# All of w_down in groups 0 to 5 by seven products, with the rows' scale put on at the residual

## The chip, the cores and the metric

The kernel runs on one core of a Trainium2 chip. The core has a TensorE (PE) for matmuls, a VectorE (DVE), a ScalarE (ACT), a GpSimd (POOL), a SyncE (SP) that issues transfers, and 16 DMA engines. The metric is the device time of one execution in microseconds (us). Three timed runs of the kernel before took 1994.78 to 1995.85 us, with a median of 1994.91.

## The reference

Two layers of a transformer-like trunk over 256 tokens (rows) of 2048 features. Each layer has an attention part and then the MLP that this change is about:

```
def rmsnorm(x, g):
    return x * lax.rsqrt(jnp.mean(x * x, axis=-1, keepdims=True) + EPS) * g

h = rmsnorm(x, norm_mlp[l])
u = jax.nn.relu(jnp.einsum('bsd,df->bsf', h, w_up[l]))        # w_up: 2048 x 8192
x = x + jnp.einsum('bsf,fd->bsd', u * u, w_down[l])           # w_down: 8192 x 2048
```

The factor rsqrt(mean + EPS), called r here, is one number per token. Since it is positive, relu(r * a) squared is r * r * relu(a) squared, so r may be applied before the square or, as its square, to any sum over the 8192 units.

## The kernel before

**Precision.** All data are float32. A weight tile is split into hi + lo: ACT casts it to a rounded form (whi, L1036), DVE subtracts that from the weights (wlo, L1037), and PE multiplies with hi and with lo. Activations are split in the same way, so a plain product of a tile takes three parts: hi x hi, lo x hi and hi x lo. All of the text calls one weight tile of 128 x 1024 numbers (512 KB) with its transfer, its cast, its DVE split and its matmuls a *step*. Three whi and three wlo buffers go round, and five for raw weights (wraw). Weight transfers are issued on SP seven steps ahead (LOOK_LOAD), splits two steps ahead (LOOK_SPLIT).

**The MLP in groups.** The 8192 units are taken in eight groups of 1024. An *up step* holds a part of w_up: eight matmuls of 128x512 with whi (L675), eight of 128x256 with wlo (L680). Four up steps make one column of 256 units, and a group has four columns, so 16 up steps, U0 to U15 below. After a column's last step `evac` in `up_steps` brings it out: ACT copies half of each bank (L653), DVE adds the other half (L654), DVE takes relu and multiplies with a row of r's (L655), ACT squares (L658) and casts (L660), DVE forms the lo part (L661). The row of r's, `rrow`, is made once per layer by `rows` in `mlp_rs`: two DVE operations, matmuls with a matrix of ones (L505) and a copy (L506). Because it comes late, a step's `post` defers the first column's evac by a step. `sums_of` makes sums and differences of the units' parts for the products (L696 to L701).

**Seven products for eight.** `strassen_steps` multiplies a group's units with two 512-column halves of w_down in the way of Strassen-Winograd: seven products P1 to P7 (in the order P1, P2, P7, P6, P5, P3, P4) of sums of weight blocks with sums of unit blocks. Every product runs over two weight tiles, called its first and second tile below; such a *product step* is six matmuls of 128x512 (L806). The operands are made in place: `on_top` is a GpSimd transfer that adds a block of w_down onto a tile in SBUF (L792), `sum_of` is a DVE sum of two tiles (L788). The tiles are `side` (four buffers), `spare` (one each of two) and `big`. DVE adds each finished bank to the residual x (L777), or subtracts it. A bank is made ready by the evacuation before: a new product can't start in a bank that is not yet added.

**Groups 0 to 5.** Columns 0 to 1023 of w_down (pair 0) are done by fourteen product steps. Columns 1024 to 2047 (pair 1) are done by seven product steps on the first tiles, and the second tiles' part by four plain *down steps* (`down_steps`) of twelve matmuls each (L468), whose banks DVE adds at L728. All of it runs beside the 16 up steps of the next group. The list `order` sets how the two kinds (1 for w_down's products, 0 for the others) follow each other; in the group's second half the products and the others alternate, and the list ends with two of the others. Groups 6 and 7 are done otherwise and keep their form.

**What sets the order on an engine.** Each engine executes its instructions in a fixed order, made when the program is built from the order in which the code issues them and a scheduler's costs. Waits between engines are semaphores. POOL issues the accumulating transfers one after the other: a later one waits while an earlier one is waiting for its tile.

Of the kernel before, what the change touches and what calls it, by code (L numbers as in the profile page):

```python
# [25 lines left out]
L = 2  # L26
# [17 lines left out]
def tile_trunk(ctx: ExitStack, tc: tile.TileContext, x_in, xt_in, w_in, w_o, w_up, w_down,  # L44
# [4 lines left out]
    D_X, D_S, D_SS, D_T, D_PV, D_QK, D_RQ, D_RK, D_SQ, D_R = 6.0, 6.0, 7.0, 18.0, 6.0, 6.0, 24.0, 16.0, 6.0, 4.0  # L49
# [52 lines left out]
    rrow = cp.tile([P, 256], F32, name="rrow")  # L102
# [350 lines left out]
    class Step:  # L453


        def __init__(self, src, kk, n, pre, mm, fourth=True, loads=None, prep=None, raw=None, post=None,
                     look=LOOK_PREP):
            self.look = look
            self.src, self.kk, self.n, self.pre, self.mm, self.fourth = src, kk, n, pre, mm, fourth
            self.loads, self.prep, self.raw, self.post = loads or [], prep, raw, post  # L460
# [27 lines left out]
    def layer_steps(l):  # L488
# [6 lines left out]
        def mlp_rs():  # L495
            r = rsqrt(mean_eps(st["ss2"], 4, 1.0 / D), 2)

            def rows():

                dg = mid(F32, 2, P)  # L500
                for t in range(NT):
                    nc.vector.tensor_scalar(dg[:, t, :], ident, r[:, t:t + 1], None, op0=ALU.mult)
                ps = tr_bank()
                for t in range(NT):
                    nc.tensor.matmul(ps[:, t * P:(t + 1) * P], full, dg[:, t, :], start=True, stop=True)  # L505
                nc.vector.tensor_copy(rrow, ps[:, 0:256])  # L506
                flags.add(("rrow", l))
            add(rows, 0.45, delay=D_R, front=True)
# [133 lines left out]
        def up_steps(g):  # L642

            out_, evacs = [], []
            for q in range(4 * g, 4 * g + 4):
                box = {}

                def evac(q=q, box=box):
                    need(("rrow", l))
                    a = mid(F32, 2, 256)  # L650
                    for i in range(2):
# [3 lines left out]
                    nc.vector.scalar_tensor_tensor(  # L655
                        a, a, 0.0, rrow.rearrange("p (o c) -> p o c", o=1).to_broadcast([P, 2, 256]),
                        op0=ALU.max, op1=ALU.mult)
# [7 lines left out]
                for s in range(4):  # L665
# [3 lines left out]
                    def mm(wh, wl, s=s, q=q, box=box, evac=evac):  # L669
# [12 lines left out]
                        if s == 3 and q > 0:  # L682
                            evac()

                    out_.append(Step(w_up[l, q * 4 + s], 4, 256, pre, mm, fourth=False,
                                     post=evacs[0] if (q, s) == (1, 0) else None))
                    if s == 0:
                        evacs.append(evac)
# [15 lines left out]
        def down_steps(gs, j, ks=range(4), shared=None):  # L704

            out_, box = [], {}
            tiles = [(g, k) for g in gs for k in ks]  # L710
# [525 lines left out]
```

## Time and profile before

| | |
|---|---|
| median of three runs | 1994.91 us |
| the profiled execution | 1995.7 us |
| its span | 1993.9 us |
| one group of 0 to 5 in the trace | 84.57 to 84.69 us |
| up steps, product steps and plain down steps in it | 16, 21, 4 |

The page of the profile gives for each engine its busy time, the share of the span and the number of instructions; PEld is PE's loading of weights, which overlaps its matmuls. A row of a timeline gives the start in us from the span's start, the duration, the engine, line and operation, output<-input with the buffers' names, and in brackets the idle time before it and what ended that. A row of a group has its count after the x, and then the sum in us, the mean in ns of one, and the idle time before it. Instructions overlap their neighbours a little, so that what one costs on its engine is read from start to start.

### The profile page before, as it was taken

How to read it: one execution, taken by the hardware profiler on the slowest of the kernel's cores; microseconds unless marked ns; L12 is line 12 of the kernel's file. 1: busy time of each engine (PE TensorE's matmuls, PEld its weight loads, DVE VectorE, ACT ScalarE, POOL GpSimd, SP SyncE). 2: the span in 40 equal slices, each digit the busy share in tenths (PEclk: the TensorE clock that was granted, in tenths of full speed). 3: DMA queues.
4: the chain of work that ended last, by engine and by line, in shares of the span. 5: the costliest groups of instructions: out<-in, count | busy, mean ns of one | idle time of the engine just before them, and what ended most of it. 6: DMA issues, size and time to landing. Idle time of an engine off the chain costs nothing.

```text
span 1993.9 us, 28351 instructions
## 1 busy us (share of the span) xinstructions
PE 1980.3 (99%) x10134; PEld 1683.2 (84%) x10134; DVE 1647.0 (83%) x2197; ACT 1247.4 (63%) x1778; POOL 396.4 (20%) x462
## 2 busy tenths in 40 slices
PE   9999999999999999999999999999999999999998
PEld 7888888888888888888888888888888888888887
DVE  6777877888888888888857678778988988888887
ACT  7667756666565656566656677566666656656664
POOL 0674620001010010100008745201010001101000
PEclk9999999999999999999999999999999999999999
DMA  9755755888888888978666467568898988989884
GB/s 341 212 164 153 235 168 190 224 260 260 252 256 243 273 248 251 273 224 252 207 190 201 153 177 222 169 190 251 233 273 243 269 248 247 265 252 260 238 264 126
DMA packets 128635, 456.31 MB, mean 229 GB/s; under 512 B 14660, under 2 KB 16964, under 8 KB 128493
## 3 DMA queue, kind: packets, MB, share of 16 engines
q1 hardware_dynamic: 109052, 384.18, 56.4%
q0 software_dynamic: 19008, 69.21, 20.1%
q8 instruction: 80, 1.31, 0.3%
q10 hardware_dynamic: 432, 1.10, 0.1%
q14 instruction: 63, 0.51, 0.1%
HBM read 448.65 MB, written 2.11 MB: 226 GB/s over the span
## 4 chain that ended last, share of the span: by engine, by line
PE 96%; DVE 1%; DMA 1%; ACT 1%; issue 1%; SPq 0%; POOL 0%; POOLq 0%; DVEq 0%; ACTq 0%
PE mm L468 32%; PE mm L675 23%; PE S L806 18%; PE mm L680 12%; PE mm L806 3%; PE S L468 2%; PE tr L380 1%; PE tr L399 1%; DMA wraw<-in_w_in_dram 1%; PE S L343 1%; PE S L342 1%; PE tr L223 1%; DVE wlo L1037 0%; ACT big L360 0%; PE tr L392 0%
## 5 line engine op out<-in xcount | busy, mean ns | idle before, releaser
L1037 DVE TENSOR_TENSOR wlo<-wraw,whi 128x1024 fp32r<-128x1024 f32 (+1 forms) x517 | 634.3, 1233 | 200.9 <-ACT whi L1036 191.4
L1036 ACT CAST whi<-wraw 128x1024 fp32r<-128x1024 f32 (+1 forms) x517 | 541.2, 1051 | 360.2 <-PE mm L675 100.2
L675 PE MATMUL mm<-big,whi 128*128 128x512 f32 x2048 | 514.1, 390 | 0.0
L468 PE MATMUL mm<-whi,big 128*128 128x512 f32 (+1 forms) x1692 | 500.1, 384 | 0.8 <-ACT whi L1036 0.8
L675 PEld LDWEIGHTS mm<-big,whi 128*128 128x128 f32 x2048 | 380.5, 188 | 79.4 <-ACT whi L1036 2.2
L468 PEld LDWEIGHTS mm<-whi,big 128*128 128x128 f32 x1692 | 314.3, 188 | 61.8 <-ACT whi L1036 1.9
L680 PEld LDWEIGHTS mm<-big,wlo 128*128 128x128 f32 x2048 | 280.9, 190 | 21.2
L468 PE MATMUL mm<-wlo,big 128*128 128x512 f32 (+1 forms) x846 | 293.3, 382 | 0.0
L806 PE MATMUL S<-whi,big 128*128 128x512 f32 x1056 | 290.1, 396 | 0.0
L680 PE MATMUL mm<-big,wlo 128*128 128x256 f32 x2048 | 287.3, 282 | 0.0
L806 PEld LDWEIGHTS S<-whi,big 128*128 128x128 f32 x1056 | 184.3, 189 | 34.2 <-DVE x L777 2.8
L468 PEld LDWEIGHTS mm<-wlo,big 128*128 128x128 f32 x846 | 159.3, 188 | 28.7
L806 PE MATMUL S<-wlo,big 128*128 128x512 f32 x528 | 163.4, 391 | 0.0
L1036 ACT CAST whi<-side 128x1024 fp32r<-128x1024 f32 x88 | 92.5, 1051 | 85.3 <-PE mm L675 76.6
L1036 ACT CAST whi<-big 128x1024 fp32r<-128x1024 f32 x88 | 92.9, 1056 | 77.5 <-DVE big L788 27.7
L468 PE MATMUL mm<-spare,big 128*128 128x512 f32 (+1 forms) x606 | 140.2, 380 | 0.0
L1037 DVE TENSOR_TENSOR wlo<-side,whi 128x1024 fp32r<-128x1024 f32 x88 | 107.7, 1224 | 35.4 <-ACT whi L1036 34.6
L792 POOL DMA_DIRECT2D spare<-in_w_down_dram x44 | 38.1, 866 | 476.2 <-DVE wlo L1037 458.4
L468 PEld LDWEIGHTS mm<-spare,big 128*128 128x128 f32 x606 | 108.9, 188 | 20.4
L1037 DVE TENSOR_TENSOR wlo<-big,whi 128x1024 fp32r<-128x1024 f32 x88 | 107.7, 1224 | 21.5 <-ACT whi L1036 21.3
L792 POOL DMA_DIRECT2D side<-in_w_down_dram x44 | 38.3, 881 | 400.9 <-DVE mid L654 150.8
L806 PEld LDWEIGHTS S<-wlo,big 128*128 128x128 f32 x528 | 99.2, 188 | 22.2
(163 smaller groups left out, 2310.3 us busy)
## 6 DMA issues: line engine op xcount, KB each, us to landing
wraw<-in_w_up_dram SPq DMA_DIRECT2D x256, 512.0 KB, 4.8
wraw<-in_w_down_dram SPq DMA_DIRECT2D x124, 512.0 KB, 5.1
wraw<-in_w_in_dram SPq DMA_DIRECT2D x119, 512.0 KB, 3.7
side<-in_w_down_dram SPq DMA_DIRECT2D x88, 512.0 KB, 5.2
wraw<-in_w_o_dram SPq DMA_DIRECT2D x64, 512.0 KB, 3.7
side<-in_w_down_dram POOLq DMA_DIRECT2D x44, 512.0 KB, 7.5
spare<-in_w_down_dram SPq DMA_DIRECT2D x44, 512.0 KB, 5.9
spare<-in_w_down_dram POOLq DMA_DIRECT2D x44, 512.0 KB, 5.5
```

The costliest lines, as they stand in the source:

```text
L223: nc.tensor.transpose(psv[:, kk, t, :], x[:, t, c0:c0 + P], ident)
L342: nc.tensor.matmul(o, st, u.kh[:, kh, :], start=True, stop=False)
L343: nc.tensor.matmul(o, st, u.kl[:, kh, :], start=False, stop=True)
L380: nc.tensor.transpose(ps[:, c * P:(c + 1) * P], u.p[:, s, kb * P:(kb + 1) * P], ident)
L399: nc.tensor.matmul(ps, u.V[:, kb, u.kv, :, :], pt[:, kb, :], start=n == 0, stop=n == 3)
L468: nc.tensor.matmul(banks[t][:, 0:n], a, (wl if part == "hl" else wh)[:, i, :], start=first and i == 0 and part == "hh", stop=last and i == ...
L675: nc.tensor.matmul(box["b"][fs], wh[:, kk, fs * P:(fs + 1) * P], ht, start=s == 0 and kk == 0, stop=False, skip_group_check=True)
L680: nc.tensor.matmul(box["b"][fs][:, 0:256], wl[:, kk, fs * P:(fs + 1) * P], ht[:, 0:256], start=False, stop=s == 3 and kk == 3, skip_group_ ...
L792: nc.gpsimd.dma_start(tile, src(par, j, h).rearrange("p (k n) -> p k n", k=2), accum_op=ALU.add)
L806: nc.tensor.matmul(o, ops[i][a], w[:, i, :], skip_group_check=True, start=fresh and h == 0 and i == 0 and a == 0 and w is wh, stop=h == ti ...
L1036: last_act[0] = nc.scalar.copy(h[:, part], w[:, part]).ins
L1037: last_lo[0] = nc.vector.tensor_sub(lo[:, part], w[:, part], f(h[:, part])).ins
```

## The change

There are two parts.

First, in groups 0 to 5 columns 1024 to 2047 are done by fourteen product steps too, for the seven product steps and the four plain steps. `_pack_down` packs the weights for it, on the host, as the packing before did for pair 0. For this second pair `moved` is empty: P7's operand, B12 + B22, is a DVE sum of two loaded tiles instead of an accumulating transfer, on both tiles. The `order` list puts a step of the other kind between the two tiles of each product but the last, and three more of them after products 1, 5 and 9 of the group.

Second, the row of r's and its matmuls are gone. The units are squared without a scale: relu moves from DVE to ACT (`AF.Relu`), the `post` deferral is dropped, and r * r, one number per row, is made once per layer on GpSimd with its negative (`r2`). Every bank of w_down is brought into the residual by `scaled_add`, x = bank * r2 + x, one DVE operation for the add or subtraction before.

```diff
         def mlp_rs():
-            r = rsqrt(mean_eps(st["ss2"], 4, 1.0 / D), 2)
-            def rows():
-                dg = mid(F32, 2, P)
-                for t in range(NT):
-                    nc.vector.tensor_scalar(dg[:, t, :], ident, r[:, t:t + 1], None, op0=ALU.mult)
-                ps = tr_bank()
-                for t in range(NT):
-                    nc.tensor.matmul(ps[:, t * P:(t + 1) * P], full, dg[:, t, :], start=True, stop=True)
-                nc.vector.tensor_copy(rrow, ps[:, 0:256])
-                flags.add(("rrow", l))
-            add(rows, 0.45, delay=D_R, front=True)
+            nc.gpsimd.tensor_tensor(r2[:, l, 0], mean_eps(st["ss2"], 4, 1.0 / D), mone[:, 0:NT], op=ALU.pow)
+            nc.gpsimd.tensor_scalar(r2[:, l, 1], r2[:, l, 0], -1.0, None, op0=ALU.mult)
...
                 def evac(q=q, box=box):
-                    need(("rrow", l))
...
-                    nc.vector.scalar_tensor_tensor(
-                        a, a, 0.0, rrow.rearrange("p (o c) -> p o c", o=1).to_broadcast([P, 2, 256]),
-                        op0=ALU.max, op1=ALU.mult)
+                    nc.scalar.activation(a, a, AF.Relu, bias=zero1[:, 0:1])
                     nc.scalar.activation(a, a, AF.Square, bias=zero1[:, 0:1])
...
+        def scaled_add(xs, bank, t, sign=1):
+            col = r2[:, l, (1 - sign) // 2, t:t + 1]
+            nc.vector.scalar_tensor_tensor(xs, bank, col, xs, op0=ALU.mult, op1=ALU.add)
...
-                xs = x[:, t, 1024 * pair + j * 512:1024 * pair + (j + 1) * 512]
-                op = nc.vector.tensor_add if sign > 0 else nc.vector.tensor_sub
-                op(xs, xs, bank)
+                scaled_add(x[:, t, 1024 * pair + j * 512:1024 * pair + (j + 1) * 512], bank, t, sign)
...
                     elif name == "P7":
+                        if h not in moved:
+                            loads = [(("B12", h), src(0, 1, h), None), (("B22", h), src(1, 1, h), None)]
+
                         def prep(h=h):
-                            on_top(raw["B12", h], 1, 1, h)
+                            if h in moved:
+                                on_top(raw["B12", h], 1, 1, h)
+                            else:
+                                sum_of(raw["B12", h], raw["B12", h], raw["B22", h])
...
             if g < 6:
-                up = up_steps(g + 1)
-                ss = up[0:4] + down_steps((g,), 3, (2, 3)) + up[4:]
-            elif g == 6:
-                ss = up_steps(7)
-            else:
-                ss = down_steps((6, 7), 2) + down_steps((6,), 3) + down_steps((7,), 3)
-            hs, _ = strassen_steps(g)
-            if g < 6:
-                more, shared = strassen_steps(g, 1, (0,), 4)
-                hs += more
-
-            if g < 6:
+                hs += strassen_steps(g, 1, ())
                 order = []
-                for p_ in range(7):
-                    order += [1, 0, 1] + [0] * (p_ in (0, 1, 2, 4))
-                order += [0, 1] * 7 + [0, 0]
-                ss += down_steps((g,), 2, (2, 3), shared)
+                for p_ in range(14):
+                    order += [1, 0, 1] if p_ < 13 else [1, 1]
+                    order += [0] * (p_ in (0, 4, 8))
```

The lines of the changed kernel that answer to those above: casts L1015, splits L1016, sums L769, accumulating transfers L773, evacuations of products L689, copies L642, adds L643, Relu L644, Square L645, cast of units L647.

Over the whole program the order listings count 72 matmuls of 128x512 and four of 128x128 fewer, 36 more casts and 36 more splits of weights, 36 more DVE sums (80 for 44), 64 Relus on ACT for 64 relu-and-scale operations on DVE, 24 evacuations of banks fewer (207 for 231), and 144 accumulating transfers for 132. Transfers issued by SP are the same in number.

Three places of the engines' orders follow. The first is ACT at the end of a group. Before, the rows run from a plain down step's cast over the copies of the last up column; `whi_5297` belongs to U0 of the next group, `spare_5189` and `spare_5224` are the two tiles of its P1:

```order
L1036 CAST whi_5265<-wraw_5176 128x1024
L653 COPY mid_5246<-mm_5125 128x256
L653 COPY mid_5246<-mm_5126 128x256
L1036 CAST whi_5279<-spare_5189 128x1024
L1036 CAST whi_5297<-wraw_5211 128x1024
L658 ACTIVATE mid_5246<-mid_5246,zero_88 128x512
L660 CAST big_5253<-mid_5246 128x512
L1036 CAST whi_5319<-spare_5224 128x1024
```

Now `big_5027` and `big_5063` are the operands of P4's two tiles, `whi_5311` belongs to U0, `spare_5218` and `spare_5243` are P1's tiles:

```order
L1015 CAST whi_5245<-big_5027 128x1024
L1015 CAST whi_5284<-big_5063 128x1024
L642 COPY mid_5265<-mm_5114 128x256
L642 COPY mid_5265<-mm_5115 128x256
L1015 CAST whi_5299<-spare_5218 128x1024
L644 ACTIVATE mid_5265<-mid_5265,zero_88 128x512
L645 ACTIVATE mid_5265<-mid_5265,zero_88 128x512
L647 CAST big_5272<-mid_5265 128x512
L1015 CAST whi_5311<-wraw_5231 128x1024
L1015 CAST whi_5326<-spare_5243 128x1024
```

U0's cast stood ahead of the Square, and now stands behind Relu, Square and the cast of the units.

The second is DVE where the second pair's P7 and P6 are prepared. Before (`side_4946` is P7's operand, `big_5072` P6's):

```order
L1037 TENSOR_TENSOR wlo_5056<-side_4946,whi_5055 128x1024
L1037 TENSOR_TENSOR wlo_5069<-wraw_4997,whi_5068 128x1024
L788 TENSOR_TENSOR big_5072<-side_5019,spare_4894 128x1024
L654 TENSOR_TENSOR mid_5090<-mid_5090,mm_4967 128x256
L654 TENSOR_TENSOR mid_5090<-mid_5090,mm_4968 128x256
L655 SCALAR_TENSOR_TENSOR mid_5090<-mid_5090,rrow 128x512
L1037 TENSOR_TENSOR wlo_5108<-big_5072,whi_5107 128x1024
```

Now (`side_4969` and `side_5007` are P7's operands, `big_5027` and `big_5063` P6's, which P4 uses later):

```order
L1016 TENSOR_TENSOR wlo_5012<-wraw_4942,whi_5011 128x1024
L769 TENSOR_TENSOR side_4969<-side_4969,side_4971 128x1024
L1016 TENSOR_TENSOR wlo_5024<-wraw_4956,whi_5023 128x1024
L769 TENSOR_TENSOR big_5027<-side_4971,spare_4842 128x1024
L1016 TENSOR_TENSOR wlo_5048<-side_4969,whi_5047 128x1024
L769 TENSOR_TENSOR side_5007<-side_5007,side_5009 128x1024
L689 SCALAR_TENSOR_TENSOR x<-mm_5016,r_83,x 128x512
L1016 TENSOR_TENSOR wlo_5060<-wraw_4994,whi_5059 128x1024
L769 TENSOR_TENSOR big_5063<-side_5009,spare_4893 128x1024
```

One sum stood there; now four stand among the splits.

The third is POOL, whose rows here are accumulating transfers alone. Before, over the end of a group:

```order
L792 DMA spare_4894<-in_w_down_dram 128x1024
L792 DMA big_5072<-in_w_down_dram 128x1024
L792 DMA spare_5189<-in_w_down_dram 128x1024
L792 DMA spare_5224<-in_w_down_dram 128x1024
L792 DMA side_5717<-in_w_down_dram 128x1024
```

Now, where `big_5805` and `big_5841` are the operands of P4's two tiles and `side_6073` and `side_6100` belong to the next group's P7:

```order
L773 DMA spare_5620<-in_w_down_dram 128x1024
L773 DMA spare_5671<-in_w_down_dram 128x1024
L773 DMA side_6073<-in_w_down_dram 128x1024
L773 DMA big_5805<-in_w_down_dram 128x1024
L773 DMA side_6100<-in_w_down_dram 128x1024
L773 DMA big_5841<-in_w_down_dram 128x1024
L773 DMA spare_5996<-in_w_down_dram 128x1024
```

The second pair's accumulations onto `big` now stand behind those onto the next group's `side` tiles.

69 lines of the change are left out of this document (32 added, 37 removed).

## The prediction

> **What bounds the kernel now.** I read the page's busy times and its chain first, then the stretches by group, then the timelines of PE, ACT and DVE at the end of a group. The page:
>
> ```profile
> PE 1980.3 (99%) x10134; PEld 1683.2 (84%) x10134; DVE 1647.0 (83%) x2197; ACT 1247.4 (63%) x1778; POOL 396.4 (20%) x462
> PE 96%; DVE 1%; DMA 1%; ACT 1%; issue 1%; SPq 0%; POOL 0%; POOLq 0%; DVEq 0%; ACTq 0%
> ```
>
> The chain that ended last is 96% matmuls. The stretches table for two of the twelve groups that the change touches (columns: busy time and count on PE, weight loads, DVE, ACT, POOL, then clock, DMA share, GB/s):
>
> ```profile
> 380.10:464.72 84.62, 84.62 (x432) 71.84 (x431) 74.43 (x94) 51.73 (x62) 7.75 (x9) 1.00 0.87 255
> 464.72:549.41 84.69, 84.69 (x432) 71.87 (x431) 74.43 (x94) 51.72 (x62) 7.77 (x9) 1.00 0.87 254
> ```
>
> PE is busy for the whole of each group at the full granted clock. So a removed matmul is worth its own time for as long as the operands keep coming. DVE has 10.2 us to spare per group and is the next bound; ACT has 33. What steps cost on PE, from the chain and the timeline of PE:
>
> ```profile
> 464.72 2.72 PE mm L468 x12
> 397.87 1.98 PE L675 MATMUL mm<-big,whi 128*128 128x512 f32 x8
> 399.68 1.11 PE L680 MATMUL mm<-big,wlo 128*128 128x256 f32 x8
> 400.63 1.09 PE L806 MATMUL S<-whi,big 128*128 128x512 f32 x4
> 401.56 0.62 PE L806 MATMUL S<-wlo,big 128*128 128x512 f32 x2
> 402.02 1.29 PE L675 MATMUL mm<-big,whi 128*128 128x512 f32 x5
> ```
>
> A 128x512 matmul takes 2.72/12 = 0.227 us. From start to start, an up step is 1.81 (hi) + 0.95 (lo) = 2.76 us and a product step 402.02 - 400.63 = 1.39 us.
>
> **What the change removes on PE.** Per group of 0 to 5, seven product steps of six matmuls and four plain steps of twelve (90) become fourteen product steps (84): 6 x 0.227 = 1.36 us. Over 12 groups that is 16.3 us. The scale's row, once per layer, goes too:
>
> ```profile
> 325.00 0.60 PE L505 MATMUL tr<-mid,full 128*128 128x128 f32 x4
> 325.37 1.86 PE L675 MATMUL mm<-big,whi 128*128 128x512 f32 x7
> ```
>
> That is 325.37 - 325.00 = 0.37 us, twice 0.7. The group end before has a short wait, on DVE's evacuations of the plain steps' banks (PE rows, then DVE rows):
>
> ```profile
> 446.35 1.75 PE L675 MATMUL mm<-big,whi 128*128 128x512 f32 x7
> 448.05 1.20 PE L806 MATMUL S<-whi,big 128*128 128x512 f32 x4
> ...
> 449.77 1.10 PE L680 MATMUL mm<-big,wlo 128*128 128x256 f32 x8
> ...
> 447.31 0.68 DVE L728 TENSOR_TENSOR x<-x,S 128x512 f32<-128x512 f32 x1
> ```
>
> From the first to the last row of PE stand eight hi matmuls and one product step: 449.77 - 446.35 = 3.42 us, where 1.81 + 1.37 is 3.18. So 0.24 us is waiting; the product starts when the evacuation of its bank ends (447.31 + 0.68). With the plain steps gone this goes, at ten group ends (five per layer; groups 5 to 6 join differently): 2.4 us.
>
> **What it adds on DVE and ACT.** Durations, from DVE's timeline and the groups table:
>
> ```profile
> 392.54 1.22 DVE L1037 TENSOR_TENSOR wlo<-wraw,whi 128x1024 fp32r<-128x1024 f32 x1
> 393.67 0.68 DVE L777 TENSOR_TENSOR x<-x,S 128x512 f32<-128x512 f32 x1
> 394.27 1.22 DVE L1037 TENSOR_TENSOR wlo<-spare,whi 128x1024 fp32r<-128x1024 f32 x1
> ...
> 423.40 0.75 DVE L654 TENSOR_TENSOR mid<-mid,mm 128x256 f32<-128x256 f32 x2
> ...
> 310.18 1.40 DVE L633 SCALAR_TENSOR_TENSOR x<-mm,sm,x 128x512 f32<-128x512 f32 x2
> ```
> ```profile
> L788 DVE TENSOR_TENSOR big<-side,spare 128x1024 f32<-128x1024 f32 x44 | 53.6, 1219 | 0.0
> L655 DVE SCALAR_TENSOR_TENSOR mid<-mid,rrow 128x512 f32<-128x512 f32 x64 | 44.0, 687 | 0.7
> L658 ACT ACTIVATE mid<-mid,zero 128x512 f32<-128x512 f32 x64 | 46.2, 722 | 15.2 <-DVE mid L655 15.2
> ```
>
> A split occupies DVE for 393.67 - 392.54 = 1.13 us, an evacuation for 0.60; a sum has the duration of a split, so 1.13 too. The scaled evacuation is the form of L633, bank times a column plus x: it is not seen on a product's bank, but bounded by 0.60 (no dearer than the add) and by 0.70 (two in 1.40); I take 0.66. Per group: three more splits and three more sums, 6 x 1.13 = 6.8; evacuations from 16 x 0.60 to 14 x 0.66, -0.4; four Relu-and-scale operations leave, 4 x 0.60 = -2.4. Together +4.0: DVE goes from 74.4 to about 78.4 of a group of 83. On ACT three casts at 0.95 and four Relus at the Square's 0.722: +5.7, to 57 of 83. Neither bounds on average. The two GpSimd operations per layer and the removed deferral of the first evacuation are done while up steps with 2.76 us each of matmuls run; from nothing to twice 0.4 us, I take nothing.
>
> **Where a new wait comes: the end of a group.** The new order puts the last two products' steps together: P3's second tile, both tiles of P4, then the next group's first up step U0, with no up step between. On ACT, U0's cast now stands behind the Relu, the Square and the cast of the last up column; before, U0's cast stood ahead of the Square. Durations and hops, from PE's and ACT's timelines:
>
> ```profile
> 463.17 1.09 PE L806 MATMUL S<-whi,big 128*128 128x512 f32 x4
> ...
> 463.38 0.64 ACT L653 COPY mid<-mm 128x256 f32<-128x256 f32 x2
> ...
> 466.57 1.06 ACT L1036 CAST whi<-big 128x1024 fp32r<-128x1024 f32 x1 [1.22 <-PE mm L468]
> 467.52 0.72 ACT L658 ACTIVATE mid<-mid,zero 128x512 f32<-128x512 f32 x1
> 468.28 0.62 ACT L660 CAST big<-mid 128x512 fp32r<-128x512 f32 x1
> 468.81 1.05 ACT L1036 CAST whi<-wraw 128x1024 fp32r<-128x1024 f32 x1
> ```
>
> A copy starts 463.38 - 463.17 = 0.21 us after the matmuls it reads. On ACT a Square takes 0.76 to the next start, the cast of units 0.53, a cast of weights 0.95. Walk, with zero at the end of P3's first tile on PE. The last up step's lo matmuls end at 0.95; P3's second tile at 2.33, P4's two at 3.70 and 5.07 (1.37 to 1.39 each): there PE wants U0. DVE: the split for P4's first tile waits for the lo buffer that P3's first tile holds, so 0.2 to 1.34; the second tile's 1.34 to 2.47; only then the two adds of the up column, 0.75 for both, to 3.22. (The copies are done at 1.8; the adds are queued behind the splits.) ACT: Relu 3.25, Square 4.0, cast of units 4.76, U0's cast 5.29 to 6.34. PE waits 6.4 - 5.07 = 1.3 us. Behind U0's split DVE has P4's evacuation, and the next group's first product needs that bank: about 0.1 more. So 1.4 us at each of ten ends, 14 us. Bounds: nothing, if ACT gets to Relu before the splits; 1.9, if hops of 0.2 come in at three places of the chain. I take the walk, since every item of it has its row. Queued behind U0's cast on ACT is only P1's second cast, which PE wants 4.1 us later.
>
> At groups 5 to 6 the new order has two up steps in front and U0's cast ahead of the chain; I count no stall there.
>
> **The sum.** The profiled execution took 1995.7 us (span 1993.9), 0.8 over the median of 1994.91. 1995.7 - 16.3 - 0.7 - 2.4 + 14 = 1990.3; less 0.8 is 1989.5 us. Its own range, with stalls of 0.9 to 1.9 at an end: 1984.5 to 1994.5.
>
> **Rivals.**
> *Full gain.* If ACT takes U0's cast in time (the adds run ahead, or the lo buffer comes free sooner than walked), there is no stall: 1989.5 - 14 = 1975.5. For it: PE did not stall in 84.62 us of these groups but for the 0.24. Against: the order of ACT's queue, which is fixed.
>
> *A late accumulate (slower).* Each group gains one accumulating GpSimd DMA, ten for nine. The window's DMA queues and issues (median us from issue to landing at the end):
>
> ```profile
> q0 software_dynamic: 1296, 4.72, 32.4%
> side<-in_w_down_dram SPq DMA_DIRECT2D x6, 512.0 KB, 4.9
> side<-in_w_down_dram POOLq DMA_DIRECT2D x3, 512.0 KB, 8.3
> big<-in_w_down_dram POOLq DMA_DIRECT2D x3, 512.0 KB, 6.7
> ```
>
> The accumulate that makes the operand of P4's second tile is now queued on POOL behind one into the next group's side tile, whose load waits until P7's second tile is split. From there to the P4 cast PE does eight product and three up steps, 8 x 1.38 + 3 x 2.76 = 19.3 us; cast and split must lie 3.5 us ahead and P7's split lies about 1 ahead of its own, so 16.8 us. Needed: load 4.9, two issues of about 0.9, landing 6.7, three hops of 0.2 to 0.4: 14.3. The margin is 2.5 us: late from a landing of 9.2 us on, and each us beyond costs 1 us in 12 groups. One more accumulate at a ninth of 32.4% brings the DMA share from 0.87 to 0.91. A landing of 11.5 us would be 2.3 x 12 = 28 us over the forecast, less what overlaps with the stall at the end: about 2010. Against: the longest queue's median here is 8.3.
>
> *DVE's burst (slower).* The second pair's four sums (P7 and P6, both tiles) now stand within six splits. DVE there: (4 + 6) x 1.13 + 0.66 + 0.75 = 12.7 us; PE's steps for these six splits: 4 x 1.39 + 2 x 2.76 = 11.1. If DVE comes to the burst without a lead, 1.6 us per group is lost, 12 x 1.6 = 19: 2009; were all three added sums uncovered, 3 x 1.13 x 12 = 41: 2030. Against: splits run up to two steps ahead, and by my walk 0.9 us of the lead is left.
>
> *DVE as the bound throughout (slower).* If DVE's queue can't be filled beyond the share that it has now, 74.43/84.62 = 88%, then 78.4 us of work take 89.1 us per group, 4.5 more than before: 1994.9 + 12 x 4.5 = 2049. Against: PE is busy for 84.62 of 84.62, which a DVE bound would not leave. The Trainium skill, "Perfetto Trace Analysis", section "Identifying the Most-Contended Engine", states that matmul busy time is no measure of TensorE's headroom, that its weight-load share is, and that the engine with the highest occupancy is the one to relieve. By that rule DVE at 88% stands above the weight loads (71.84 of 84.62, 85%), and this rival is the likely one; the trace's matmuls end to end do not agree with it.
>
> **How the numbers follow.** Forecast 0.50, full gain 0.20, late accumulate 0.16, DVE's burst 0.11, DVE as the bound throughout 0.03. About 0.2%, 4 us, is what a measurement here can tell from no change: faster is below 1990.9, slower above 1998.9. Of the forecast 0.6 lies below 1990.9 and 0.4 within; the full gain is all faster; of the late accumulate 0.35 lies within and the rest is slower; of the burst 0.25 lies within; DVE as the bound is all slower. Faster 0.30 + 0.20 = 0.50; within 0.20 + 0.06 + 0.03 = 0.29; slower 0.10 + 0.08 + 0.03 = 0.21. The range takes in the full gain, and of the slow cases the small ones: 1974 to 2005, about 0.15 to 0.2 left out, nearly all above. The likeliest one's own range is 1984.5 to 1994.5.
>
> **What would show it.** In the changed kernel's profile: 6 matmuls fewer per group and groups of 84.62 - 1.36 - 0.24 + 1.4 = 84.4 us; PE idle some 1.3 us before the first hi matmul of a new group's first up step, its releaser ACT's cast of whi, and on ACT that cast directly behind the cast of units. No idle at that place, with groups of 83.0, is the full gain. Idle before P4's second tile, released by a cast that waited for the accumulate into big, and landings over 9.2 us, is the late accumulate. Idle in the middle of the second pair, before P7 or P6 with DVE's sums or splits as releasers, is the burst. DVE per group near 78.4, ACT near 57, and the scaled evacuation near 744 ns would bear out the sizes. A scaled evacuation of a product's bank near 1 us, or group times of 88 and more, would make the whole argument wrong.

## The result: slower by 3.9%, and the profile after

The changed kernel takes 2073.65 us (median of four runs, 2070.79 to 2078.08) against 1995.12: a ratio of 1.0393, 95% interval 1.038 to 1.0406. I had forecast 1989.5. The profiled execution took 2070.79 us, its span 2069.0. The page's busy times and chain:

```profile
PE 1992.6 (96%) x10054; PEld 1686.0 (81%) x10054; DVE 1686.8 (82%) x2175; ACT 1325.9 (64%) x1878; POOL 409.2 (20%) x476
PE 79%; DMA 11%; DVE 4%; ACT 2%; issue 2%; POOL 0%; SPq 0%; POOLq 0%; DVEq 0%; ACTq 0%
```

PE has 80 instructions fewer than before (72 matmuls of 128x512, and the scale's four of 128x128, which the trace lists as eight) and is busy for longer (1992.6 for 1980.3 us), and the chain has 11% DMA where it had 1%. The totals of the waits (time waited, times, longest):

```profile
PE S L787 <- ACT mid L644: 55.6, 10, 7.5
PE mm L662 <- ACT whi L1015: 8.0, 2, 4.3
ACT whi L1015 <- DMA big<-in_w_down_dram: 52.6, 12, 6.4
```

PE stands idle 63.6 us in twelve places, one at the end of each group of 0 to 5 of both layers, 3.7 to 7.5 us long. ACT waits at twelve places for an accumulate onto `big`. The chain through the first two of these places (start, duration, what):

```profile
424.01 4.46 DMA side<-in_w_down_dram
...
429.66 13.79 DMA big<-in_w_down_dram
...
443.53 1.05 ACT whi L1015
...
446.52 0.73 ACT mid L644
...
447.30 4.34 PE S L787 x12
...
513.98 9.21 DMA side<-in_w_down_dram
...
524.29 11.47 DMA big<-in_w_down_dram
```

Read upwards from the idle end: P4's two tiles (12 matmuls) start at 447.30. Ahead of them stands the cast of P4's second tile at 443.53, which waited for an accumulate that took 13.79 us to land. This accumulate was issued behind one onto a side tile of the next group, which itself had to wait for that tile's load (4.46 us, at the second place 9.21). At the second place this kept POOL from issuing it until 524.29, though P6's split of the same tile had ended at 519.0; at the first place it is 429.66 for 429.0, so that there nearly all of the delay is the landing. I had taken 6.7 us for the landing.

What lies between this cast and the start of P4 is on DVE:

```profile
439.77 1.23 DVE L1016 TENSOR_TENSOR wlo<-big,whi 128x1024 fp32r<-128x1024 f32 x1 [0.67 <-ACT whi L1015]
444.60 1.23 DVE L1016 TENSOR_TENSOR wlo<-big,whi 128x1024 fp32r<-128x1024 f32 x1 [3.60 <-ACT whi L1015]
445.75 0.74 DVE L643 TENSOR_TENSOR mid<-mid,mm 128x256 f32<-128x256 f32 x2
446.41 0.74 DVE L689 SCALAR_TENSOR_TENSOR x<-S,r,x 128x512 f32<-128x512 f32 x1
```

The first row is the split for P4's first tile: its operand is ready before PE falls idle at 442.0. The late accumulate belongs to the second tile alone. But at ten of the twelve places (at the two ends of group 5 an up step waits instead) PE starts the first tile only when P3's evacuation, the last row, has ended (446.41 + 0.74), and on DVE that stands behind the second tile's split and the two adds. Experiments 1, 5 and 6 show this wait. So 3.8 us of the idle time lie behind the landing at 443.5, and as much at the second place (535.75 to 539.60). Without that wait, the first tile could have run from 442.0 and the second from the end of its cast at 444.6: some 1.2 to 1.5 us idle for 5.3, by an estimate from these rows.

The second loss stands in the matmuls. Stretches around the first idle time (columns as in the prediction: busy PE, weight loads, DVE, ACT, POOL, then granted clock, DMA share, GB/s):

```profile
428.00:442.00 14.00, 14.00 (x71) 11.49 (x69) 11.37 (x12) 7.14 (x8) 1.72 (x2) 1.00 1.04 260
442.00:447.30 5.30, 0.01 (x2) 0.03 (x1) 2.70 (x5) 3.28 (x6) 0.00 (x0) 0.95 0.96 390
447.30:450.00 2.70, 2.70 (x7) 2.12 (x8) 2.50 (x5) 1.94 (x3) 0.86 (x1) 0.50 0.03 12
450.00:453.00 3.00, 3.00 (x14) 2.51 (x13) 2.15 (x3) 2.00 (x3) 0.00 (x0) 0.97 1.08 184
```

After 5.3 us without matmuls the granted clock is 0.50 for about 2.7 us: the 12 matmuls of P4 take 4.34 us, where 12 x 0.227 is 2.72. The Trainium skill, "TensorE: Matmul & The Clock Gate", section "What's actually happening", says that the gate lets half of the pulses through after at least one idle window of about 3.4 us, and that the windows run freely and don't start anew with the kernel; the 0.50 after 5.3 us agrees with that.

DMA is full ahead of the idle time (a share of 1.04 from 428 to 442), though over the whole group it is not. The accumulates and their landings there, medians of two each in the stretch from 423 to 446 us:

```profile
side<-in_w_down_dram POOLq DMA_DIRECT2D x2, 512.0 KB, 8.7
big<-in_w_down_dram POOLq DMA_DIRECT2D x2, 512.0 KB, 11.7
```

Taken one by one they are issued at 423.84 (side), 425.34 (big), 428.76 (side) and 429.66 (big), and land 7.4, 9.6, 9.9 and 13.8 us later: at 431.2, 434.9, 438.7 and 443.5. So they land in the order of issue, 3.7 to 4.8 us apart, and the fourth lands behind the three ahead.

My theory A, then: the next group's two side accumulates, which are needed only in the next group, stand ahead of the one that P4 needs, and the idle time that follows halves PE's clock on top.

### The profile page after: what moved, and what is told of

It reads as the page before. It is cut to its first block, busy times and chain, and to the rows that moved or that the text cites. A ratio compares the mean times of both kernels' runs of the same rounds, so it can differ in the third digit from the quotient of the medians.

```text
span 2069.0 us, 28502 instructions
## 1 busy us (share of the span) xinstructions
PE 1992.6 (96%) x10054; PEld 1686.0 (81%) x10054; DVE 1686.8 (82%) x2175; ACT 1325.9 (64%) x1878; POOL 409.2 (20%) x476
## 3 DMA queue, kind: packets, MB, share of 16 engines
q8 instruction: 79, 1.29, 0.3%
## 4 chain that ended last, share of the span: by engine, by line
PE 79%; DMA 11%; DVE 4%; ACT 2%; issue 2%; POOL 0%; SPq 0%; POOLq 0%; DVEq 0%; ACTq 0%
PE mm L468 24%; PE mm L662 19%; PE S L787 18%; PE mm L667 10%; DMA big<-in_w_down_dram 7%; PE mm L787 4%; DVE wlo L1016 2%; DMA side<-in_w_down_dram 2%; PE tr L380 1%; DMA wraw<-in_w_in_dram 1%; ACT whi L1015 1%; PE tr L399 1%; ACT big L360 1%; PE S L343 1%; PE S L342 1%
## 5 line engine op out<-in xcount | busy, mean ns | idle before, releaser
L1016 DVE TENSOR_TENSOR wlo<-wraw,whi 128x1024 fp32r<-128x1024 f32 (+1 forms) x481 | 590.4, 1234 | 187.8 <-ACT whi L1015 183.8
L1015 ACT CAST whi<-wraw 128x1024 fp32r<-128x1024 f32 (+1 forms) x481 | 501.6, 1048 | 335.9 <-PE mm L662 116.6
L787 PE MATMUL S<-whi,big 128*128 128x512 f32 x1344 | 386.1, 410 | 55.6 <-ACT mid L644 55.6
L468 PE MATMUL mm<-whi,big 128*128 128x512 f32 (+1 forms) x1404 | 423.9, 384 | 0.3 <-ACT whi L1015 0.3
L787 PEld LDWEIGHTS S<-whi,big 128*128 128x128 f32 x1344 | 246.3, 197 | 107.7 <-ACT mid L644 59.5
L468 PEld LDWEIGHTS mm<-whi,big 128*128 128x128 f32 x1404 | 260.5, 189 | 49.9 <-ACT whi L1015 1.2
L468 PE MATMUL mm<-wlo,big 128*128 128x512 f32 (+1 forms) x702 | 253.0, 381 | 0.0
L787 PE MATMUL S<-wlo,big 128*128 128x512 f32 x672 | 215.6, 403 | 0.0
L773 POOL DMA_DIRECT2D spare<-in_w_down_dram x56 | 48.4, 865 | 727.6 <-DVE wlo L1016 714.7
L1016 DVE TENSOR_TENSOR wlo<-big,whi 128x1024 fp32r<-128x1024 f32 x112 | 136.7, 1220 | 65.9 <-ACT whi L1015 65.9
L1015 ACT CAST whi<-side 128x1024 fp32r<-128x1024 f32 x112 | 117.9, 1053 | 100.3 <-PE mm L662 50.2
L1015 ACT CAST whi<-big 128x1024 fp32r<-128x1024 f32 x112 | 117.7, 1051 | 97.6 <-DMA big<-in_w_down_dram 52.6
L1016 DVE TENSOR_TENSOR wlo<-side,whi 128x1024 fp32r<-128x1024 f32 x112 | 136.6, 1219 | 27.5 <-ACT whi L1015 16.1
L1015 ACT CAST whi<-spare 128x1024 fp32r<-128x1024 f32 x112 | 117.4, 1049 | 52.3 <-PE S L787 27.0
L1016 DVE TENSOR_TENSOR wlo<-spare,whi 128x1024 fp32r<-128x1024 f32 x112 | 136.7, 1220 | 10.0 <-ACT whi L1015 6.1
```

The lines of the kernel that those rows point to most:

```text
L468: nc.tensor.matmul(banks[t][:, 0:n], a, (wl if part == "hl" else wh)[:, i, :], start=first and i == 0 and part == "hh", stop=last and i == ...
L773: nc.gpsimd.dma_start(tile, src(par, j, h).rearrange("p (k n) -> p k n", k=2), accum_op=ALU.add)
L787: nc.tensor.matmul(o, ops[i][a], w[:, i, :], skip_group_check=True, start=fresh and h == 0 and i == 0 and a == 0 and w is wh, stop=h == 1 ...
L1015: last_act[0] = nc.scalar.copy(h[:, part], w[:, part]).ins
L1016: last_lo[0] = nc.vector.tensor_sub(lo[:, part], w[:, part], f(h[:, part])).ins
```

## Experiments

**1. The side accumulates behind the big ones.** One edge in the order on POOL:

```diff
                         def prep(h=h):
                             if h in moved:
-                                on_top(raw["B12", h], 1, 1, h)
+                                with tc.issue_after(last_big[0]) if last_big[0] is not None else nullcontext():
+                                    on_top(raw["B12", h], 1, 1, h)
...
-                            on_top(t2[h], 1, 0, h)
+                            last_big[0] = on_top(t2[h], 1, 0, h)
```

> The changed kernel, with one difference: on POOL the next group's two accumulates onto side tiles are issued behind the two accumulates that make P4's operands (big), instead of among them. In the changed kernel's trace the second big accumulate lands 11 to 14 us after its issue, PE then stands idle 4.3 to 7.5 us at each of 12 group ends (63.6 us in all) and its matmuls after that take 29 us more than their number would need. Theory A (the side accumulates stand in the way, in POOL's queue and in the DMA engines): the landing falls to 7 to 9 us, the idle time at a group end to 0 to 1.5 us, and the time to 1980 to 1997 us. Theory B (the DMA engines are full at that place whatever is issued first): landing stays at 11 us or more, the idle time at 4 us or more, the time above 2050 us.

Measured 1997.84 us, ratio to the kernel before 1.001 (1.000 to 1.002): 75.8 us less by the order of two transfers. Theory A holds, B falls. The page, the same stretch's accumulates, and PE's waits:

```profile
PE 1966.1 (99%) x10054; PEld 1667.2 (84%) x10054; DVE 1682.6 (84%) x2175; ACT 1326.1 (66%) x1878; POOL 409.3 (21%) x476
```
```profile
big<-in_w_down_dram POOLq DMA_DIRECT2D x2, 512.0 KB, 7.0
...
side<-in_w_down_dram POOLq DMA_DIRECT2D x2, 512.0 KB, 12.7
```
```profile
PE S L788 <- ACT mid L645: 15.9, 10, 1.6
```

Big and side have changed places: the last two in the row land late, now the ones that nobody waits for. The second big accumulate is issued at 429.44, much as before (429.66), and lands after 6.5 us instead of 13.8. The spans differ by 73.1 us: idle time on PE fell from 63.6 to 17 us (10 x 1.6 and 2 x 0.7 at the ends of group 5), 46 us, and PE's busy time by 1992.6 - 1966.1 = 26.5 us, which is the halved clock: the count of matmuls is the same, the mean clock goes from 0.982 to 0.999, and what the granted clock lacks of 1.00 in the 9 us after each of the twelve idle times adds up to 28 us in the changed kernel's trace.

What is left is 1.6 us at each of ten group ends, and it isn't where I had forecast it. PE, DVE and ACT there:

```profile
439.32 1.12 PE L668 MATMUL mm<-big,wlo 128*128 128x256 f32 x8
...
441.20 0.62 PE L788 MATMUL S<-wlo,big 128*128 128x512 f32 x2
443.41 1.17 PE L788 MATMUL S<-whi,big 128*128 128x512 f32 x4 [1.58 <-ACT mid L645]
```
```profile
439.58 2.36 DVE L1018 TENSOR_TENSOR wlo<-big,whi 128x1024 fp32r<-128x1024 f32 x2 [0.67 <-ACT whi L1017]
441.85 0.75 DVE L644 TENSOR_TENSOR mid<-mid,mm 128x256 f32<-128x256 f32 x2
442.52 0.75 DVE L690 SCALAR_TENSOR_TENSOR x<-S,r,x 128x512 f32<-128x512 f32 x1
```
```profile
444.14 0.62 ACT L648 CAST big<-mid 128x512 fp32r<-128x512 f32 x1
444.67 1.04 ACT L1017 CAST whi<-wraw 128x1024 fp32r<-128x1024 f32 x1
```

PE waits ahead of P4's first tile, not ahead of U0, and starts (443.41) when DVE's evacuation of P3 (L690) has ended at 443.27. The row names the Relu, which P4 does not need; it merely ends about then, at 443.35. In the program P4's first matmul does wait for P3's evacuation: P3's bank and P4's are halves of one tile `S`, and the waits are set by tile. In experiment 5 the row names this evacuation, and experiment 6 takes the wait away. On DVE this evacuation is behind both splits of P4 and the two adds of the last up column.

**2. Without the late accumulates.**

```diff
-                            on_top(t2[h], 1, 0, h)
+                            if not pair:
+                                on_top(t2[h], 1, 0, h)
```

> The changed kernel without the second pair's accumulates onto big: P4's operand there is left without one of its blocks, so two of ten accumulates of a group, and that part of the product, are left out. Theory A or B (the late accumulate is all of it): no idle time over 1.5 us at group ends, 1978 to 1995 us; what is left there is then the end-of-group chain on ACT and DVE that I forecast at 1.4 us. Rival C (the order of P4's steps behind P3's evacuation and behind P4's second split on DVE is what stops PE, the landing only comes beside it): idle 3 us or more stays at a group end, 2030 us or more.

Measured 1998.15 us (ratio 1.0013, 1.0002 to 1.0023), the time of experiment 1. So all of the loss above that goes with the late accumulates, as A and B have it; but the residue is 1.60 us at each end and the time 3 us over what I allowed, and it is rival C's mechanism at a smaller size: the order behind P3's evacuation.

**3. An up step moved to the group's end.**

```diff
-                    order += [0] * (p_ in (0, 4, 8))
+                    order += [0] * (p_ in (4, 8, 12))
```

> The changed kernel with one up step of a group moved from behind its first product to behind its thirteenth, so that an up step stands between P3 and P4: P4's second tile is wanted 2.76 us later. Theory A or B: the idle time at a group end falls by about 2.8 us, from 5.3 to 2.5 us, and with it the slow matmuls; 2025 to 2045 us. If instead the transfers shift with the steps (each is issued when a step before is split), the landing shifts along and the time stays within 15 us of 2073.65.

Measured 2011.63 us (1.0079, 1.0059 to 1.0099): 13 us below the range that I expected. The halved clock goes whole (the mean clock is 0.999), and no wait of PE's at the group ends is over 0.9 us. PE's busy time, 1977.3 us, is still 11 us above experiment 1's, which I did not follow. ACT still waits 43.6 us for the accumulates, but PE has work meanwhile. Several waits of 0.4 to 0.6 us come up instead, one in each group before an up step's lo matmuls with DVE's split as releaser (4.5 us in all). It stands behind the second pair's sums and splits on DVE, as the burst of the prediction's rival would:

```profile
424.29 1.10 PE L667 MATMUL mm<-big,wlo 128*128 128x256 f32 x7 [0.38 <-DVE wlo L1016]
444.32 1.20 PE L787 MATMUL S<-whi,big 128*128 128x512 f32 x4 [0.62 <-ACT whi L1015]
446.76 1.87 PE L662 MATMUL mm<-big,whi 128*128 128x512 f32 x7 [0.44 <-ACT whi L1015]
449.17 1.20 PE L787 MATMUL S<-whi,big 128*128 128x512 f32 x4 [0.55 <-DVE x L689]
```

**4. The scale alone.** The kernel before, with its own products and order list, and of the change only the pieces on `mlp_rs`, `evac` and `scaled_add`, in short:

```diff
-                    nc.vector.scalar_tensor_tensor(a, a, 0.0, <the row of r's>, op0=ALU.max, op1=ALU.mult)
+                    nc.scalar.activation(a, a, AF.Relu, bias=zero1[:, 0:1])
...
-                op(xs, xs, bank)
+                scaled_add(x[:, t, 1024 * pair + j * 512:1024 * pair + (j + 1) * 512], bank, t, sign)
```

> The kernel before with the second part alone: units squared unscaled, Relu on ACT, banks scaled where they are added; the plain down steps and seven product steps of columns 1024 to 2047 stay. By the sums of the prediction: 0.7 us less on PE, DVE 1.4 us less per group, ACT 2.9 us more, no new wait: 1992 to 1996 us. Rival: the Relu in front of the Square makes the evacuation of an up column so late that product steps wait for their units: over 2000 us, with idle time on PE whose releaser is ACT's cast of units or DVE's sums.

Measured 1991.96 us, ratio 0.9981 (0.9972 to 0.999): a gain of some 3.9 us, just under the low edge of what I expected. In the trace the first layer's MLP is 2.4 us shorter and the second's 1.1. The matmuls of the row are 0.37 of each; where the rest comes from I did not follow. The Relu in front of the Square does no harm in this order.

**5. The products alone.** The changed kernel with the row of r's, relu on DVE and the deferred first evacuation as before, and so without the scale in `scaled_add`; of the edit, this piece:

```diff
-            nc.vector.scalar_tensor_tensor(xs, bank, col, xs, op0=ALU.mult, op1=ALU.add)
+            (nc.vector.tensor_add if sign > 0 else nc.vector.tensor_sub)(xs, xs, bank)
```

> The changed kernel with the first part alone: fourteen product steps, and the scale's row with relu on DVE as before. POOL has the same order as in the changed kernel, the side accumulates among the big ones. If the late accumulate explains the loss, it is all here: 2065 to 2085 us, with PE idle 4 us or more at group ends. If the scale part (Relu ahead of the Square on ACT) was needed for the stall: below 2040 us.

Measured 2076.94 us (1.0407, 1.0386 to 1.0427): the whole loss is in the products' part. Relu is on DVE here, behind P3's evacuation, and the row of PE's wait names the evacuation (L706):

```profile
448.62 1.84 PE L804 MATMUL S<-whi,big 128*128 128x512 f32 x4 [4.09 <-DVE x L706]
```

**6. A bank of its own for P7 and P4,** on top of experiment 1:

```diff
-                            box["a"], box["d"] = two[:, 0], two[:, 1]
+                            box["a"] = two[:, 0]
                         if (name, h) == ("P2", 0):
                             box["b"] = mm_bank()
+                        if (name, h) == ("P7", 0):
+                            box["d"] = mm_bank()
```

> As the run with the side accumulates behind the big ones, and with P7's and P4's bank allocated by itself instead of as half of one tile with the bank of P1, P6, P5 and P3. So P4's first tile does not wait for P3's evacuation, which in that run's trace stands on DVE behind P4's second split and two adds and kept PE waiting 1.58 to 1.75 us at ten group ends. If my forecast's chain holds (U0's cast on ACT behind Relu, Square and the cast of units), the wait then moves to the next group's first up step, 1.0 to 1.5 us with releaser ACT's cast, groups stay at 84.4 to 84.9 us, and the time is 1990 to 1997 us. If that chain had slack, there is no wait at the group's end, groups of 83.1 to 83.4 us, and 1974 to 1981 us.

Measured 1979.21 us, ratio 0.9918 (0.9902 to 0.9935): the second of the two outcomes. The wait for P3's evacuation goes and no other of its size takes its place:

```profile
441.71 1.07 PE L790 MATMUL mm<-whi,big 128*128 128x512 f32 x4
...
444.44 1.07 PE L790 MATMUL S<-whi,big 128*128 128x512 f32 x4
...
445.80 1.98 PE L663 MATMUL mm<-big,whi 128*128 128x512 f32 x8
```

With the bank free, the order changed too: the next group's P1 goes ahead of U0 on PE (444.44, then 445.80), and U0's cast ahead of the Square on ACT (at 443.31). So my forecast's chain is not tested by this run, only avoided. What the separate bank alone would do, with the side accumulates still ahead, no run shows.

**7 and 8. An up step between the tiles of every product,** on top of experiment 1, in two forms:

```diff
-                    order += [1, 0, 1] if p_ < 13 else [1, 1]
-                    order += [0] * (p_ in (0, 4, 8))
+                    order += [1, 0, 0, 1] if p_ == 0 else [1, 0, 1]     # 8: [1, 0, 1] for all
+                    order += [0] * (p_ in (9,))                         # 8: (4, 9)
```

> The side accumulates behind the big ones, and another order list: an up step between the two tiles of every product, the last too, two between the first product's, and one more behind the tenth product. No two products' tiles then stand together without an up step's matmuls near, so that evacuations, splits and the last up column have 2.76 us more. If what is left at the group's end is only order (P3's evacuation and the ACT chain): no idle time above 0.2 us there, groups of 83.0 to 83.4 us, 1972 to 1980 us. If DVE's share (78 us of 83) is what limits: waits of 0.4 us and more come up elsewhere, before product steps or lo matmuls with DVE's split as releaser, groups of 84 us or more, over 1985 us.

> The same, but one up step between the first product's tiles like everywhere, and the second extra one behind the fifth product. The last up column of a group must then be copied, added, rectified, squared, cast and split in about 5.5 us of PE's work before the next group's first product takes its second tile; the operations alone take 4.3 us by the rows of before. If the queues add 1 to 2 us: idle time of 0.3 to 1 us before that step with DVE's or ACT's units as releaser, 1976 to 1992 us. If not, the same time as the run before within 3 us.

Measured 1979.06 us (0.9916, 0.9901 to 0.9931) and 1979.77 us (0.9919, 0.9904 to 0.9934). The idle times at the group ends are gone in both. DVE does not limit at 77.8 us of 83.0, as a stretch of about one group's length in experiment 7 shows, and the last up column is in time in experiment 8 too:

```profile
441.00:524.00 83.00, 83.00 (x425) 70.32 (x424) 77.81 (x93) 57.26 (x69) 8.69 (x10) 1.00 0.90 264
```

**9 and 10. Does the idle time itself slow the matmuls after it?** The changed kernel, with matmuls on zeros in the idle time, 12 and then 20:

```diff
+                        if pair and (name, h) == ("P4", 0):
+                            idle_bank = mm_bank()
+                            with tc.issue_after(box["last"]):
+                                for _ in range(12):        # 10: 20
+                                    keep = nc.tensor.matmul(idle_bank, warm[:, 0:P], warm, start=True, stop=True).ins
+                            hold = tc.issue_after(keep)
```

> The changed kernel with 12 matmuls of 128x512 more in each of the twelve groups, on zeros into a bank that nobody reads, placed on PE between P3's second and P4's first tile, where PE stands idle 4.3 to 7.5 us. They need 12 x 0.227 = 2.7 us of that, and leave gaps of 1.6 to 4.8 us. In the changed kernel the granted clock is 0.50 for some 3 us after those idle times, and PE's busy time is 26.5 us higher than in the run with the side accumulates behind the big ones, where idle times are 1.58 us and the clock stays at 1.00. If the length of the idle time lowers the clock: added work makes the kernel faster, by 15 to 27 us, 2047 to 2060 us. If the idle time costs only itself: 2071 to 2078 us, as without them.

> The same with 20 matmuls, 4.5 us of the idle time, gaps of 0 to 3 us left. If the idle time lowers the clock: 2045 to 2052 us (the 26.5 us all gone, and 0 to 0.3 us per group added where the gap is shorter than the filling). If not: 2071 to 2080 us.

With 12: 2057.81 us (1.0311, 1.0291 to 1.0332). The kernel does 144 matmuls more, 33 us of PE's time, and is 15.8 us faster. PE's busy time of 2010.9 less 32.7 is 1978.2, where the changed kernel has 1992.6: 14 of the 26.5 us are gone. Gaps of 1.2 to 3.9 us are left, and they don't act by length alone:

```profile
537.32 1.17 PE L796 MATMUL S<-whi,big 128*128 128x512 f32 x4 [3.45 <-ACT mid L644]
...
894.19 2.04 PE L796 MATMUL S<-whi,big 128*128 128x512 f32 x4 [2.76 <-ACT mid L644]
...
1557.29 1.17 PE L796 MATMUL S<-whi,big 128*128 128x512 f32 x4 [3.01 <-ACT mid L644]
```

Four matmuls take 2.04 us after a gap of 2.76 (the granted clock is 0.52 over the 3 us from 894.19), and 1.17 after one of 3.01, with the clock at 1.00. After the 3.45 they take 1.17 too, but there the clock halves some 1.4 us later (0.73 over the 3 us from 537.32). In all, half the clock follows six of the twelve gaps, of 2.53 to 3.94 us, and not those of 2.59 and 3.01 us. By the Trainium skill's freely running windows (the section named above), it would depend on where in a window a gap falls. That short and long are mixed here agrees with it, but the windows themselves no run shows. Gaps of 2.53 to 2.76 us are shorter than that section's 3.4 us and halved the clock all the same, and there the measurement decides.

With 20 it is 2072.29 us (1.0384, 1.0363 to 1.0405), not the 2045 to 2052 that I expected; it lies in the range that I had given for the other outcome. The mean clock is 0.998, so that part of the reason holds. But these matmuls also moved what comes after them:

```profile
448.48 1.17 PE L796 MATMUL S<-whi,big 128*128 128x512 f32 x4 [0.85 <-ACT mid L644]
452.75 1.67 PE L662 MATMUL mm<-big,whi 128*128 128x512 f32 x6 [1.26 <-ACT whi L1024]
```
```profile
447.71 0.72 ACT L644 ACTIVATE mid<-mid,zero 128x512 f32<-128x512 f32 x1 [0.45 <-DVE mid L643]
448.46 0.73 ACT L645 ACTIVATE mid<-mid,zero 128x512 f32<-128x512 f32 x1
449.22 0.62 ACT L647 CAST big<-mid 128x512 fp32r<-128x512 f32 x1
451.13 0.62 ACT L683 CAST big<-mid 128x512 fp32r<-128x512 f32 x1 [1.29 <-DVE mid L681]
451.65 1.04 ACT L1024 CAST whi<-wraw 128x1024 fp32r<-128x1024 f32 x1
```

U0's first matmuls wait 1.26 us for their cast, at the place and of the length that I had forecast, but by another path. In this order U0's cast (451.65) stands also behind the cast of the sums, L683, which it did not in my walk, and that waits 1.29 us for DVE. With nothing between, U0's cast could follow the cast of the units at 449.8 and end near 450.9, before PE wants it at 451.5 (an estimate from these rows). The wait comes at ten group ends, 12.7 us. The rest of the difference from what I expected I leave open.

**11. The order list alone,** that of experiment 7, with the side accumulates still ahead:

> The changed kernel with the other order list alone (two up steps between the first product's tiles, one between every other's, one more behind the tenth product); on POOL the side accumulates stay ahead of the big ones. P4's second tile is then wanted 5.5 us later than in the changed kernel, seen from P6's splits. If the accumulate's lateness is a matter of that distance: the idle time of 5.3 us goes, 1977 to 1990 us. If accumulates that land one after the other (about 4 us apart in the changed kernel's trace) simply need more than there is: idle times of 2 us or more stay at the group ends, over 2010 us.

Measured 2027.08 us (1.0157, 1.0137 to 1.0178): the second outcome. PE still waits 31.5 us in eleven places, up to 4.8 us, and the clock halves again, once after a gap of only 2.06 us:

```profile
1624.67 3.68 PE L662 MATMUL mm<-big,whi 128*128 128x512 f32 x8 [2.06 <-ACT whi L1015]
```

The granted clock is 0.52 over the 3 us from there. So 5.5 us more distance takes away 46.6 of the 78.5 us lost but doesn't mend it alone; with the order on POOL changed too (experiment 7) it is mended.

**12. All three,** the edits of experiments 1, 6 and 7 together:

> The three remedies together: side accumulates behind the big ones, P7's and P4's bank by itself, an up step between the tiles of every product. The runs with two of them each have groups of 83.0 us with PE busy throughout, so nothing is left at the group ends: 1977 to 1981 us, the same as each within 2 us. If the weight loads' waits for P3's and P5's evacuations (5.2 us in all in the run with steps between) still cost: 1972 to 1976 us.

Measured 1973.94 us, ratio to the kernel before 0.9892 (0.9875 to 0.9908), 1.1% faster and the best of all. It falls into the second of the expected ranges, with the weight loads' waits for evacuations down to 1.4 us (5.2 in experiment 7). Those for an up step's splits, 4.2 us in experiment 7, are gone from the table. That these waits are the cause is likely by the size, but no run tells one from the other.

## Why the prediction was wrong

*PE's saving: right.* With nothing in the way the kernel is at 1973.94, where the full gain was put at 1975.5, and groups take 82.9 us (from one group's row to the next group's in experiment 12), where 83.0 were worked out.

*Sizes on DVE and ACT: right.* 78.35 to 78.44 us of DVE per group in the changed kernel for 78.4, and 57.5 of ACT for some 57; the scaled evacuation has a mean of 747 ns for 744; the DMA share is 0.90 where nothing is late, for 0.91.

*The forecast's term of 14 us for the group end: the size near, the place wrong.* The step that failed is the walk's "P4's two at 3.70 and 5.07": it lets P4's first tile follow P3's second at once. P4 waits for P3's evacuation, because the two banks are one tile, and DVE has that evacuation behind the splits and adds of the same walk. Experiment 1 shows this wait at 1.58 us, ten times. ACT's half of the walk came out: in experiment 1 U0's cast directly follows the cast of the units and ends at 445.71, 6.4 us after P3's first tile (439.32), where the walk has 6.34. But PE comes 1.75 us later than walked and finds it done. Once the bank is separate the next P1 goes first, and the wait is hidden again. So the forecast wait itself is shown by no run; the one of 1.26 us in experiment 10 has its length by another path. That 14 us came near what is there (17 us) is luck.

*The late accumulate: the cause right, the price and the path wrong, and the chance of 0.16 too low.* I had worked out that a landing of over 9.2 us is late, and that each us beyond costs 1 us in 12 groups. The step that failed is "Needed: load 4.9, two issues of about 0.9, landing 6.7". The 6.7 was the median of accumulates that mostly had no other ahead of them, taken for one that now stands behind others: in the first group shown three are issued within 6 us ahead of it, the four land about 4 us apart, and it took 13.8 us. In the second it took 11.5, and the side tile's load 9.21 for 4.9. "Against: the longest queue's median here is 8.3" was a number of the old order. With 13.8 my own rule gives 4.6 x 12 = 55 us over the forecast, 2045. That this is near the idle time measured is in part luck, for the rule had the path wrong too. It lets the late tile hold up P4's second tile alone, and PE stands idle ahead of the first: the step is again "P4's two at 3.70 and 5.07". How much of the 63.6 us is due to the shared tile is open, since no run separates the banks and leaves POOL's order as it is.

*What no rival had: the clock.* The idle times were 63.6 us; 26.5 us more went into matmuls at half the clock. I priced every wait at its own length.

*DVE's burst and DVE as the bound: not the cause.* In the changed kernel's table of waits TensorE's matmuls have none for DVE's splits, and its weight loads 0.2 us; what looks like the burst, 0.38 us per group, comes in experiment 3. In experiment 7 PE is busy for 83.0 of 83.0 us with DVE at 94%: that kernel runs DVE fuller than before, and is faster, so DVE's 88% was no bound. The section of the Trainium skill, "Perfetto Trace Analysis", that the prediction cites for this rival names MFU, the share of peak arithmetic, beside the weight loads as the measure of TensorE. The prediction left that out, so it did not test the section's whole rule, and no run here does.

## What to carry to other kernels

An order of transfers on one queue is a schedule: read which of them someone waits for soon, and put those first. When the order changes, a median landing from the old trace is no price; count what stands ahead in the queue. Here waits of 3.7 to 7.5 us on TensorE cost more than their length, and a false wait, from two banks that share one tile, passed the lateness of one operand on to matmuls that did not need it.

## What was not expected of the hardware

Four accumulating transfers of 512 KB, issued within 5.8 us, landed in the order of issue and 3.7 to 4.8 us apart, the last after 13.8 us. Each of the twelve idle times of PE of 3.7 to 7.5 us was followed by half the granted clock, for 2.9 to 6.2 us of the matmuls behind it, and 33 us of matmuls on zeros, put into them, made the kernel 15.8 us faster (2073.65 to 2057.81). The shortest idle time seen with half the clock behind it is 2.06 us (experiment 11), the longest without is 3.01 us (experiment 9).
